# Strassen operand rings of their own, output weights loaded first, and attention's loads issued by POOL

## The chip, the cores and the metric

The kernel runs on one core of a Trainium2 chip. The metric is the device time of one execution in microseconds, as the median of several. One launch computes the whole block in float32. Engines are named as in the profile: PE (TensorE), DVE (VectorE), ACT (ScalarE), POOL (GpSimd), SP (SyncE, which here only issues DMAs).

## The reference

2048 rows of width 1024 pass through one block: normalization, one input projection to q, k, v (8 heads of 64) and u, vg, then stick-breaking attention beside a gated unit, normalization of each half, the output projection with a residual, and an MLP of width 4096 with squared relu.

```
h = rmsnorm(x, norm_mix_g);  q, k, v, u, vg = split(h @ w_in)
a_out = stick_breaking_attention(q, k, v)     # A[t,s] = sigmoid(z_ts) * prod_{s<j<t} (1 - sigmoid(z_tj))
b_out = spatial_gating(gelu(u), gelu(vg), sg_ln_g, sg_ln_b, sg_w, sg_b)
mix = concat(rmsnorm(a_out, g[:512]), rmsnorm(b_out, g[512:]))
x = x + mix @ w_out
x = x + square(relu(rmsnorm(x, norm_mlp_g) @ w_up)) @ w_down
return rmsnorm(x, norm_final_g)
```

## The kernel before

The rows are worked in four chunks of 512. Every float32 product is made of three passes: `split` (L78 to L85) turns an operand into a high part (ACT copies it, L81) and a low part (DVE subtracts, L82), and `mm3` (L87 to L91) issues high by high, high by low and low by high as 128 x 128 by 128 x 512 matmuls. These are called main matmuls below.

The stages follow each other: the projection of chunks 0 and 1 (to about 280 us), of chunks 2 and 3 (to 612), Out(0) and Out(1) (to 830), the up projection of chunks 0 and 1 by plain products (to 1340), Out(2) (to 1480), the plain down projection of chunks 0 and 1 with Out(3) beside its end (to 1930), and then chunks 2 and 3 by Strassen's seven products, up (to about 2262) and down (to the end).

Attention is a generator (`attention`, L316 to L411) that is dealt out beside the other stages by `together` at fixed rates, from 280 us on. It has 80 units (chunk, head, segment of keys) of four steps. Each step weighs one block (two score matmuls, L345 and L346, and on the diagonal a mask, L348; two sigmoids on ACT; a scan L359 and a product L360 on DVE), turns an earlier one (transposes L370 and a split) and gathers a still earlier one (value matmuls L388 and L389). At the first step of a unit it loads keys (two DMAs, L329), values (L331) and on the diagonal queries (L334), all issued by SP, into rings of 2, 3 and 2 buffers.

`Out` makes a chunk's output projection: `operands` (L465) loads attention's output a_d and the gated half b_d, takes both sums of squares, scales b's rows on ACT so that one factor serves both halves, and transposes b; `weights` (L506) loads a quarter of w_out, splits it and, for chunk 0, the product stores it split; `product` (L521) runs 8 x 3 main matmuls into each of 8 banks, which L543 adds to the residual; `turn` (L552) normalizes and transposes for the MLP.

In the Strassen part `Rights` and `Lefts` make the operands of the up products, and `down_seven` (L818 on) those of the down products: 4 groups of 7 products of 48 main matmuls; each product loads its left operand from s_d (L857), splits two left and two right operands and is added from four banks by L828, in the last group also by L831. All of these tiles, raw and split, share one ring `w8` of nine buffers; weights of odd groups take some of them too.

The scheduler fixes the order of each engine's and each queue's instructions when the kernel is built, from the order of the code, its own estimates and the buffers that are free. Each engine and each queue then runs in that order: what stands behind a waiting DMA on SP waits too.

Of the kernel before, what the change touches and what calls it, by code (L numbers as in the profile page):

```python
# [16 lines left out]
P = 128  # L17
# [17 lines left out]
def block_kernel(ctx: ExitStack, tc: tile.TileContext, x, x_t, gmix, w_in, ln_g, ln_b, sgw, sgb,  # L35
# [280 lines left out]
    def attention(cs):  # L316
# [4 lines left out]
        def weigh(u, tb):  # L321
# [4 lines left out]
            if tb == 0:  # L326
                kt = att.tile([P, 2, TC], F32R, name="kt", bufs=2)
                for j in range(2):
                    nc.sync.dma_start(kt[j * HD:(j + 1) * HD].bitcast(F32), k_d[h, :, :, ss].rearrange("x d t -> d x t"))  # L329
                vt = att.tile([P, NTB, 2 * HD], F32R, name="vt", bufs=3)  # L330
                nc.sync.dma_start(vt.bitcast(F32), v_d[seg, h].rearrange("p n x d -> p n (x d)"))  # L331
                if diag:
                    qt = att.tile([P, TC], F32R, name="qt", bufs=2)
                    nc.sync.dma_start(qt.bitcast(F32), q_d[h].rearrange("x d t -> (x d) t")[:, tcs])  # L334
                    carry = [None] * NTB
                else:
                    qt, carry = state[u - 1][2:4]
                state[u] = [kt, vt, qt, carry, []]
# [85 lines left out]
    class Room:  # L424
# [11 lines left out]

        def raw8(self, shape):
            return self.get("w8", shape)

# [19 lines left out]
    class Out:  # L459
# [5 lines left out]
        def operands(self):  # L465

            rm, c = self.rm, self.c
            at = rm.t8([4, TC])
            nc.sync.dma_start(at, a_d[:, c * TC:(c + 1) * TC].rearrange("(n p) t -> p n t", p=P))
            st = rm.t8([4, SBW])  # L470
            nc.sync.dma_start(st, b_d[c * TC:(c + 1) * TC, :].rearrange("(n p) d -> p n d", p=P))
            ssq = rm.small("rb_ssq", NTB)
            for tb in range(NTB):
                sq = rm.t4([SBW], BF16)
                nc.scalar.activation(sq, st[:, tb, :], AF.Square, accum_out=ssq[:, tb:tb + 1])
            am = self.am = rm.pair([4, TC])
            split4(am, at)
            yield
            nc.scalar.activation(at, at, AF.Square)
            total = rm.pool.tile([P, TC], F32, name="a_sq", bufs=1)  # L480
            nc.gpsimd.tensor_tensor(at[:, 0:2, :], at[:, 0:2, :], at[:, 2:4, :], ALU.add)
            nc.gpsimd.tensor_tensor(total, at[:, 0, :], at[:, 1, :], ALU.add)
            rb = rsqrt_mean(rm.pool, ssq, NTB, SBW, "rb")
            pssq = rm.ps()
            for tb in range(NTB):
                nc.tensor.matmul(pssq[:, tb:tb + 1], total[:, tb * P:(tb + 1) * P], ones, start=True, stop=True)
            m = rm.small("ra_m", NTB)
            nc.vector.tensor_scalar(m, pssq[:, :NTB], 1.0 / SBW, EPS, ALU.mult, ALU.add)
            ra = rm.small("ra", NTB)
            nc.gpsimd.tensor_tensor(ra, m, mhalf[:, :NTB], ALU.pow)  # L490
            root = rm.small("ra_root", NTB)
            nc.gpsimd.tensor_tensor(root, m, ra, ALU.mult)
            nc.gpsimd.tensor_tensor(rb, rb, root, ALU.mult)
            self.ras = [ra[:, tb:tb + 1] for tb in range(NTB)]
            yield
            bm = self.bm = rm.pair([4, TC])
            for tb in range(NTB):
# [6 lines left out]
                yield  # L504

        def weights(self, half, part):  # L506
# [14 lines left out]
        def product(self):  # L521
            rm, c = self.rm, self.c
            self.ys = []
            for t2 in range(2):
                y = rm.t8([2, D])
                r0 = c * TC + t2 * 2 * P
                nc.sync.dma_start(y, x[r0:r0 + 2 * P, :].rearrange("(n p) d -> p n d", p=P))
                self.ys += [y[:, 0, :], y[:, 1, :]]
            ys = self.ys

            for half in range(2):
                ws = [self.weights(half, part) for part in range(2)]
                hs = slice(half * 512, (half + 1) * 512)
                for tb in range(NTB):
                    ts_ = slice(tb * P, (tb + 1) * P)
                    ps = rm.ps()
                    for part, m in ((0, self.am), (1, self.bm)):
                        for e in range(4):
                            mm3(ps, m[0][:, e, ts_], m[1][:, e, ts_], ws[part][0][:, e, :], ws[part][1][:, e, :],
                                part == 0 and e == 0, part == 1 and e == 3)  # L540
                            if e == 1 or part == 0 and e == 3:
                                yield
                    nc.vector.scalar_tensor_tensor(ys[tb][:, hs], ps, self.ras[tb], ys[tb][:, hs], ALU.mult, ALU.add)  # L543
                    if half == 1:
                        nc.sync.dma_start(y_d[c][:, tb, :], ys[tb])
                    yield
                if c == 0:
                    for part in range(2):
                        for i in range(2):
                            nc.sync.dma_start(wo_d[half, part, i], ws[part][i].bitcast(F32))  # L550

# [124 lines left out]
    class Rights:  # L676


        def __init__(self, rm):

            self.rm, self.hc = rm, [None] * 7
            self.b11, self.t2, self.b12, self.b21, self.b22 = (rm.raw8([4, TC]) for _ in range(5))
# [28 lines left out]
    class Lefts:  # L711


        def __init__(self, rm, q):
            self.rm, self.pair, self.n = rm, None, 0
            st = rm.raw8([2, 2, 512])
# [77 lines left out]
    class Down:  # L794
# [260 lines left out]
```

## Time and profile before

| | us |
|---|---|
| median of 3 runs | 2624.02 |
| lowest and highest run | 2620.88, 2625.3 |
| the profiled execution | 2620.27 |
| its span | 2618.6 |
| busy: PE, DVE, ACT, POOL | 2454.1, 1684.6, 1158.5, 315.4 |

The span is the time from the first to the last instruction of the profiled execution; 1.7 us of its time lie around it. Busy time is what an engine's instructions cover. A matmul's record is longer than the distance to the next one, since they are pipelined.

### The profile page before, as it was taken

The page shows a single profiled execution, that of the slowest core. Times are in us where ns is not written, and L with a number is a line of the kernel's source. Part 1 is how long each engine was busy: PE and PEld are TensorE (multiplying, and loading weights), DVE is VectorE, ACT ScalarE, POOL GpSimd, SP SyncE. Part 2 cuts the span into 40 slices and gives each one's busy share as a digit, 9 for nine tenths or more (in the row PEclk, how much of TensorE's full clock was granted, in tenths as well). Part 3 has the DMA queues.
Part 4 walks back from the last instruction along what each step waited for, and adds up shares of the span by engine and source line. Part 5 has one row for each costly group of instructions (what it writes and reads, how often), then busy time and mean ns, then how long its engine had stood idle before and what let it go on. Part 6 is the DMA issues. An engine that isn't in the chain of part 4 may idle for free. (4 is left out here: it accounts for less than half of the span.)

```text
span 2618.6 us, 30138 instructions
## 1 busy us (share of the span) xinstructions
PE 2454.1 (94%) x11328; PEld 1985.7 (76%) x11328; DVE 1684.6 (64%) x2236; ACT 1158.5 (44%) x2020; POOL 315.4 (12%) x259
## 2 busy tenths in 40 slices
PE   8899898997979999999999899999989999799997
PEld 7787677775757888888877688788767888687875
DVE  3643557868675666666666688635566665468877
ACT  4422335536454555555564454313134544233333
POOL 1100000101010000000010000000023323213330
PEclk9999999998989999999999899999999999999998
DMA  9637788677654343333364633346223344753332
GB/s 374 244 125 219 215 255 261 205 221 224 244 190 157 121 121 121 121 124 122 121 236 162 197 121 113 122 156 241 96 81 142 140 161 149 261 206 116 113 113 113
DMA packets 158225, 446.58 MB, mean 171 GB/s; under 512 B 12544, under 2 KB 28928, under 8 KB 138624
## 3 DMA queue, kind: packets, MB, share of 16 engines
q1 hardware_dynamic: 149744, 417.39, 47.8%
q0 software_dynamic: 4032, 25.17, 2.4%
q10 hardware_dynamic: 4304, 2.10, 0.3%
q8 instruction: 90, 1.47, 0.2%
q14 instruction: 55, 0.45, 0.1%
HBM read 314.59 MB, written 130.02 MB: 170 GB/s over the span
## 5 line engine op out<-in xcount | busy, mean ns | idle before, releaser
L89 PE MATMUL mm<-t,t 128*128 128x512 f32 x1280 | 499.5, 394 | 4.5 <-DVE t L664 4.5
L91 PE MATMUL mm<-t,t 128*128 128x512 f32 x1280 | 502.3, 393 | 0.0
L90 PE MATMUL mm<-t,t 128*128 128x512 f32 x1280 | 501.9, 392 | 0.3 <-DVE t L82 0.3
L359 DVE TENSOR_TENSOR_SCAN pr<-kk,pr,zeros 128x513 f32<-128x513 f32 x192 | 248.3, 1293 | 117.3 <-ACT kk L351 116.9
L351 ACT ACTIVATE kk<-z 128x512 f32<-128x512 f32 (+2 forms) x320 | 171.5, 536 | 334.5 <-PE z L346 187.8
L89 PEld LDWEIGHTS mm<-t,t 128*128 128x128 f32 x1280 | 242.3, 190 | 55.6 <-DVE t L664 4.9
L90 PEld LDWEIGHTS mm<-t,t 128*128 128x128 f32 x1280 | 241.9, 189 | 51.4 <-DVE t L82 1.1
L91 PEld LDWEIGHTS mm<-t,t 128*128 128x128 f32 x1280 | 241.5, 189 | 51.6
L81 ACT ACTIVATE w<-w 128x512 fp32r<-128x512 f32 (+1 forms) x150 | 121.1, 825 | 299.6 <-DMA w<-s_d 172.3
L82 DVE TENSOR_TENSOR w<-w,w 128x512 fp32r<-128x512 f32 (+1 forms) x150 | 176.5, 1191 | 88.7 <-ACT w L81 86.8
L370 PE MATMUL tr<-ident,b 128*128 128x128 f32 x1088 | 186.3, 283 | 43.7 <-DVE aT L82 30.0
L90 PE MATMUL mm<-w,w 128*128 128x512 f32 x512 | 204.1, 399 | 17.3 <-DVE w L82 17.3
L82 DVE TENSOR_TENSOR aT<-tr,aT 128x512 fp32r<-128x512 f32 (+1 forms) x320 | 190.9, 599 | 35.7 <-ACT aT L81 35.6
L89 PE MATMUL mm<-w,w 128*128 128x512 f32 x512 | 201.4, 396 | 12.4 <-ACT w L81 11.5
L81 ACT ACTIVATE aT<-tr 128x512 fp32r<-128x512 f32 (+1 forms) x320 | 172.6, 541 | 90.2 <-PE tr L370 89.7
L91 PE MATMUL mm<-w,w 128*128 128x512 f32 x512 | 202.8, 396 | 0.0
L370 PEld LDWEIGHTS tr<-ident,b 128*128 128x128 f32 x1088 | 133.6, 144 | 90.7 <-DVE aT L82 38.8
L81 ACT ACTIVATE t<-t 128x1024 fp32r<-128x1024 f32 x104 | 105.7, 1060 | 179.1 <-DMA t<-in_w_down 112.8
L353 ACT ACTIVATE b<-z 128x512 f32<-128x512 f32 (+2 forms) x320 | 171.3, 535 | 0.5 <-PE tr L370 0.5
L356 DVE TENSOR_TENSOR_SCAN pr<-kk,zeros 128x128 f32<-128x128 f32 (+3 forms) x128 | 105.5, 826 | 90.8 <-ACT kk L351 90.3
L89 PE MATMUL mm<-t,w 128*128 128x512 f32 x384 | 154.0, 401 | 8.9 <-DVE acts L775 4.7
L388 PE MATMUL av<-aT,vt 128*128 128x512 f32 (+1 forms) x320 | 144.5, 452 | 13.7 <-DMA vt<-v_d 3.5
(192 smaller groups left out, 4629.3 us busy)
## 6 DMA issues: line engine op xcount, KB each, us to landing
w_in<-wi_d SPq DMA_DIRECT2D x40, 1024.0 KB, 8.0
kt<-k_d SPq DMA_DIRECT2D x160, 256.0 KB, 4.9
t<-in_w_down SPq DMA_DIRECT2D x28, 1024.0 KB, 6.6
s_d<-acts SPq DMA_DIRECT2D x16, 1792.0 KB, 6.2
w<-s_d SPq DMA_DIRECT2D x28, 1024.0 KB, 4.8
t<-wo_d SPq DMA_DIRECT2D x24, 1024.0 KB, 8.7
wi_d<-w_in POOLq DMA_DIRECT2D x20, 1024.0 KB, 8.0
vt<-v_d SPq DMA_DIRECT2D x80, 256.0 KB, 2.9
```

What stands on the lines that cost most here:

```text
L81: nc.scalar.activation(hi, src, AF.Copy)
L82: nc.vector.tensor_tensor(lo, src, hi.bitcast(F32), ALU.subtract)
L89: nc.tensor.matmul(ps, lh, rh, start=first, stop=False, skip_group_check=more)
L90: nc.tensor.matmul(ps, lh, rl, start=False, stop=False, skip_group_check=more)
L91: nc.tensor.matmul(ps, ll, rh, start=False, stop=last, skip_group_check=more)
L351: nc.scalar.activation(kk[:, :L], z[:, :L], AF.Sigmoid, scale=-QK_SCALE)
L353: nc.scalar.activation(b[:, :L], z[:, :L], AF.Sigmoid, scale=QK_SCALE)
L356: nc.vector.tensor_tensor_scan(pr[:, L - 1::-1], kk[:, L - 1::-1], zeros[:, :L], 1.0, ALU.mult, ALU.add)
L359: nc.vector.tensor_tensor_scan(pr[:, ::-1], kk[:, ::-1], zeros, carry[tb], ALU.mult, ALU.add)
L370: nc.tensor.transpose(tr[:, tb * P:(tb + 1) * P], bs[tb][:, j * P:(j + 1) * P], ident)
L388: nc.tensor.matmul(av[:, t0:], vt[:, j, :], aT[:, 0, t0:], start=first, stop=False)
```

## The change

Three edits, and all that the scheduler makes of them.

Attention's loads go from `nc.sync` to `nc.gpsimd`. In `Out`, the first quarter of the weights is loaded before the operands, b is transposed as it is and its row factors are applied at the eviction, so that the product has four groups of four banks (half 0 of b, half 0 of a, half 1 of b, half 1 of a); a's sum of squares is taken by 16 small matmuls instead of additions on POOL and 4 of them. In the Strassen part the ring of nine becomes three: `w8` of 5, `raw8` of 2 for loads that are still to be split, and `x8` of 2.

```diff
@@ attention, weigh
-                    nc.sync.dma_start(kt[j * HD:(j + 1) * HD].bitcast(F32), k_d[h, :, :, ss].rearrange("x d t -> d x t"))
+                    nc.gpsimd.dma_start(kt[j * HD:(j + 1) * HD].bitcast(F32), k_d[h, :, :, ss].rearrange("x d t -> d x t"))
...
-                nc.sync.dma_start(vt.bitcast(F32), v_d[seg, h].rearrange("p n x d -> p n (x d)"))
+                nc.gpsimd.dma_start(vt.bitcast(F32), v_d[seg, h].rearrange("p n x d -> p n (x d)"))
...
-                    nc.sync.dma_start(qt.bitcast(F32), q_d[h].rearrange("x d t -> (x d) t")[:, tcs])
+                    nc.gpsimd.dma_start(qt.bitcast(F32), q_d[h].rearrange("x d t -> (x d) t")[:, tcs])
@@ Room
-        def raw8(self, shape):
-            return self.get("w8", shape)
+        def raw8(self, shape, dtype=F32):
+            return self.get("raw8", shape, dtype)
+
+        def x8(self, shape, dtype=F32R):
+            return self.get("x8", shape, dtype)
@@ Out.operands
+            self.rbs = []
+            self.ready = [self.weights(0, 1)]
+            st = rm.t8([4, SBW])
+            nc.sync.dma_start(st, b_d[c * TC:(c + 1) * TC, :].rearrange("(n p) d -> p n d", p=P))
...
+                m = rm.small("rb_m", NTB)
+                nc.vector.tensor_scalar(m, ssq, 1.0 / SBW, EPS, ALU.mult, ALU.add)
+                rb = rm.small("rb", bufs=2 * NTB)
+                nc.gpsimd.tensor_tensor(rb, m, mhalf[:, 0:1], ALU.pow)
+                self.rbs.append(rb)
...
-            nc.gpsimd.tensor_tensor(at[:, 0:2, :], at[:, 0:2, :], at[:, 2:4, :], ALU.add)
-            nc.gpsimd.tensor_tensor(total, at[:, 0, :], at[:, 1, :], ALU.add)
...
-                nc.scalar.activation(st[:, tb, :], st[:, tb, :], AF.Copy, scale=rb[:, tb:tb + 1])
...
+            for tb in range(NTB):
+                for e in range(4):
+                    nc.tensor.matmul(pssq[:, tb:tb + 1], at[:, e, tb * P:(tb + 1) * P], ones, start=e == 0, stop=e == 3)
+            ra = rsqrt_mean(rm.pool, pssq[:, :NTB], NTB, SBW, "ra")
@@ Out.product
+            def group(half, part, m, rr):
+                ws = self.ready.pop() if self.ready else self.weights(half, part)
...
+                    for e in range(4):
+                        mm3(ps, m[0][:, e, ts_], m[1][:, e, ts_], ws[0][:, e, :], ws[1][:, e, :], e == 0, e == 3)
...
+                    nc.vector.scalar_tensor_tensor(ys[tb][:, hs], ps, rr[tb], ys[tb][:, hs], ALU.mult, ALU.add)
...
+            yield from group(0, 1, self.bm, self.rbs)
+            yield from group(0, 0, self.am, self.ras)
+            yield from group(1, 1, self.bm, self.rbs)
+            yield from group(1, 0, self.am, self.ras)
@@ Rights
-            self.keep(0, b11, rm.w8)
+            self.keep(0, b11, rm.x8)
@@ Lefts.operand
-                self.pair = self.rm.w8([2, 2, 512])
+                self.pair = self.rm.raw8([2, 2, 512], F32R) if self.first and self.n == 0 else self.rm.w8([2, 2, 512])
@@ Down.load
-                    st = self.rm.raw8([4, 512]) if g % 2 and h else self.rm.t8([4, 512])
+                    st = self.rm.x8([4, 512], F32) if g % 2 and h else self.rm.t8([4, 512])
@@ block_kernel
-    rm = Room(None, None, dict(w8=9, s12=1, t8=12, acts=2, t2=2), dict(w8=hx, s12=hx))
+    rm = Room(None, None, dict(w8=5, raw8=2, x8=2, s12=1, t8=12, acts=2, t2=2),
+              dict(w8=hx, raw8=hx, x8=hx, s12=hx))
```

PE, in the projection of chunk 2, at attention's fourth to sixth step (a name is the tile written, then the tiles read; z are scores, tr the transposes, av the values, mm a main bank). Before:

```order
L388 MATMUL av<-aT,vt 128x256
L389 MATMUL av<-aT,vt 128x256
L345 MATMUL z<-kt,qt 128x256
L346 MATMUL z<-kt,qt 128x256
L348 LDWEIGHTS ident_b
L348 MATMUL z<-neg_b,ident_b 128x128
L345 MATMUL z<-kt,qt 128x256
L346 MATMUL z<-kt,qt 128x256
```

With the change, two steps on:

```order
L348 LDWEIGHTS ident_b
L348 MATMUL z<-neg_b,ident_b 128x128
L370 MATMUL tr<-ident,b 128x128 x4
L388 MATMUL av<-aT,vt 128x256
L389 MATMUL av<-aT,vt 128x256
L89 MATMUL mm<-hT,w_in 128x512
L90 MATMUL mm<-hT,w_in 128x512
L91 MATMUL mm<-hT,w_in 128x512
```

Before, the score matmuls of one step follow those of the last with no main matmul between, and 64 of them come in one block after the eighth step; now 12 stand in most steps (here the first three of six, the other six behind the next step's scores). Counted over the whole order: of the 80 steps that lie beside the projection, 35 had none or almost none and 8 have none now; of the 49 up to the end of Out(1) it is 43 and 33; of those about Out(2) it is 17 and 23.

SP, at the seam between the Strassen stages (s_d are the left operands of the down products, stored by L587 or L586; in_w_down its weights; y_d the residual). Before, buffer numbers kept:

```order
L857 DMA w_18012<-s_d_97 128x2048
L808 DMA t_17985<-in_w_down 128x4x512
L587 DMA s_d_100<-acts 128x7x512
L808 DMA t_17987<-in_w_down 128x4x512
L808 DMA t_17989<-in_w_down 128x4x512
L808 DMA t_17991<-in_w_down 128x4x512
L819 DMA t_18001<-y_d_89 128x2048
L587 DMA s_d_100<-acts 128x7x512
L819 DMA t_18002<-y_d_89 128x2048
L819 DMA t_18005<-y_d_90 128x2048
L819 DMA t_18006<-y_d_90 128x2048
L857 DMA w_18088<-s_d_97 128x2048
```

With the change:

```order
L856 DMA raw_18144<-s_d_97 128x2048
L586 DMA s_d_100<-acts 128x7x512
L856 DMA raw_18220<-s_d_97 128x2048
L807 DMA x_18634<-in_w_down 128x4x512
L586 DMA s_d_100<-acts 128x7x512
L807 DMA t_18117<-in_w_down 128x4x512
L807 DMA t_18119<-in_w_down 128x4x512
L807 DMA t_18121<-in_w_down 128x4x512
L807 DMA t_18123<-in_w_down 128x4x512
L818 DMA t_18133<-y_d_89 128x2048
L586 DMA s_d_100<-acts 128x7x512
L818 DMA t_18134<-y_d_89 128x2048
```

Before, one load of a down product's operand (from s_d_97) stands ahead of the weights and y, now two, with one load of group 1's weights (x_18634) behind them.

DVE, in the first half of the Strassen down stage (w are split operands, raw the loaded ones; L828 or L827 adds a finished product's four banks). Before, buffer numbers kept:

```order
L82 TENSOR_TENSOR w_18598<-acts,w_18598 128x1024
L82 TENSOR_TENSOR w_18655<-w_18653,w_18655 128x1024
L82 TENSOR_TENSOR w_18658<-t_18498,w_18658 128x1024
L82 TENSOR_TENSOR w_18662<-w_18653,w_18662 128x1024
L82 TENSOR_TENSOR w_18665<-w_18502,w_18665 128x1024
L828 TENSOR_TENSOR t_18009<-mm,t_18009 128x512 x4
L82 TENSOR_TENSOR w_18727<-w_18721,w_18727 128x1024
```

With the change:

```order
L82 TENSOR_TENSOR w_18657<-x_18634,w_18657 128x1024
L82 TENSOR_TENSOR w_18721<-raw_18715,w_18721 128x1024
L82 TENSOR_TENSOR w_18724<-acts,w_18724 128x1024
L82 TENSOR_TENSOR w_18727<-raw_18715,w_18727 128x1024
L827 TENSOR_TENSOR t_18141<-mm,t_18141 128x512 x4
L82 TENSOR_TENSOR w_18730<-acts,w_18730 128x1024
L82 TENSOR_TENSOR w_18787<-raw_18785,w_18787 128x1024
L82 TENSOR_TENSOR w_18790<-t_18630,w_18790 128x1024
```

Before, the number of splits between one product's additions and the next's varies, and often all four of the next product stand ahead of the additions; now the additions of a product always stand ahead of the fourth split of the next.

## Rows read from the trace of the kernel before

**Rows 1.** The page, part 1: engine, busy us, share of the span, instructions.
```profile
PE 2454.1 (94%) x11328; PEld 1985.7 (76%) x11328; DVE 1684.6 (64%) x2236; ACT 1158.5 (44%) x2020; POOL 315.4 (12%) x259
```

**Rows 2.** Six stretches: ends and length, busy us of PE, PEld, DVE, ACT, POOL, clock, DMA share, GB/s.
```profile
280.00:480.00 200.00, 178.12 (x853) 138.10 (x852) 129.96 (x233) 92.38 (x201) 15.97 (x20) 0.97 0.79 244
480.00:612.00 132.00, 128.92 (x661) 105.88 (x661) 95.92 (x148) 59.45 (x123) 5.59 (x5) 1.00 0.70 204
612.00:830.00 218.00, 181.43 (x847) 140.05 (x846) 148.36 (x216) 110.84 (x224) 21.14 (x23) 0.89 0.65 217
830.00:1340.00 510.00, 507.37 (x2496) 417.40 (x2495) 334.94 (x425) 293.14 (x555) 12.79 (x13) 1.00 0.40 123
1340.00:1480.00 140.00, 119.64 (x575) 92.87 (x574) 98.83 (x128) 68.42 (x130) 9.36 (x11) 0.94 0.67 229
2262.00:2300.00 38.00, 22.09 (x73) 16.72 (x72) 20.07 (x18) 10.32 (x12) 16.47 (x7) 0.73 0.69 267
```

**Rows 3.** PE timeline at 662 us: start, duration, instruction.
```profile
661.97 0.39 PE L89 MATMUL mm<-t,t 128*128 128x512 f32 x1
662.20 0.39 PE L90 MATMUL mm<-t,t 128*128 128x512 f32 x1
```

**Rows 4.** Groups by line and shape, DVE: busy us, mean ns, idle before.
```profile
L359 DVE TENSOR_TENSOR_SCAN pr<-kk,pr,zeros 128x513 f32<-128x513 f32 x192 | 248.3, 1293 | 117.3 <-ACT kk L351 116.9
L82 DVE TENSOR_TENSOR aT<-tr,aT 128x512 fp32r<-128x512 f32 x224 | 152.4, 681 | 25.5 <-ACT aT L81 25.4
L360 DVE TENSOR_TENSOR b<-b,pr 128x512 f32<-128x512 f32 x192 | 132.9, 692 | 10.7
```

**Rows 5.** PE waits of 612 to 830 us: total us, times, longest.
```profile
PE mm L501 <- ACT t L498: 4.1, 4, 1.5
...
PE mm L486 <- POOL a_sq L482: 2.0, 1, 2.0
```

**Rows 6.** PE timeline at 637 us; below it the DVE group of the product's eviction.
```profile
637.30 0.95 PE L486 MATMUL mm<-ones,a_sq 128*128 128x1 f32 x8
L543 DVE SCALAR_TENSOR_TENSOR t<-mm,ra,t 128x512 f32<-128x512 f32 x32 | 24.0, 749 | 67.8 <-PE mm L91 60.2 <-issue 7.7
```

**Rows 7.** PE waits of 1340 to 1480 us.
```profile
PE av L388 <- DMA vt<-v_d: 3.5, 1, 3.5
```

**Rows 8.** PE waits of 2262 to 2300 us, and of 2300 to 2618 us.
```profile
PE mm L89 <- ACT w L81: 11.5, 1, 11.5
PE mm L90 <- DVE w L82: 12.9, 6, 7.3
```

**Rows 9.** SP timeline at the seam: start, duration, DMAs issued.
```profile
2236.96 0.34 SPq L857 DMA_DIRECT2D w<-s_d  x1
...
2250.15 6.90 SPq L808 DMA_DIRECT2D t<-in_w_down  x3
...
2272.64 2.99 SPq L819 DMA_DIRECT2D t<-y_d  x3
2275.68 25.96 SPq L857 DMA_DIRECT2D w<-s_d  x3
```

**Rows 10.** Groups by line and shape, DVE in the Strassen stages.
```profile
L82 DVE TENSOR_TENSOR w<-w,w 128x1024 fp32r<-128x1024 f32 x70 | 103.6, 1493 | 61.0 <-ACT w L81 61.0
...
L828 DVE TENSOR_TENSOR t<-mm,t 128x512 f32<-128x512 f32 x104 | 67.5, 684 | 16.5 <-PE mm L91 16.5
```

**Rows 11.** Queue waits of SP, whole span: total us, times, longest.
```profile
SPq L331 <- PE av L389: 330.2, 52, 12.6
```

**Rows 12.** POOL groups by line, and page part 6: KB each, us to landing.
```profile
L126 POOL DMA_DIRECT2D wi_d<-w_in x20 | 11.0, 551 | 133.0 <-DVE w_in L82 133.0
w_in<-wi_d SPq DMA_DIRECT2D x40, 1024.0 KB, 8.0
...
wi_d<-w_in POOLq DMA_DIRECT2D x20, 1024.0 KB, 8.0
```

More of the change, by code (lines that the diff above doesn't have):

```diff
@@ L467, in operands @@
             rm, c = self.rm, self.c
+            self.rbs = []
+            self.ready = [self.weights(0, 1)]
+            st = rm.t8([4, SBW])
+            nc.sync.dma_start(st, b_d[c * TC:(c + 1) * TC, :].rearrange("(n p) d -> p n d", p=P))
             at = rm.t8([4, TC])
             nc.sync.dma_start(at, a_d[:, c * TC:(c + 1) * TC].rearrange("(n p) t -> p n t", p=P))
-            st = rm.t8([4, SBW])
-            nc.sync.dma_start(st, b_d[c * TC:(c + 1) * TC, :].rearrange("(n p) d -> p n d", p=P))
@@ L472, in operands @@
-            ssq = rm.small("rb_ssq", NTB)
+            bm = self.bm = rm.pair([4, TC])
             for tb in range(NTB):
                 sq = rm.t4([SBW], BF16)
[L475 to L480, printed above, removed]
-            nc.gpsimd.tensor_tensor(at[:, 0:2, :], at[:, 0:2, :], at[:, 2:4, :], ALU.add)
@@ L482, in operands @@
-            nc.gpsimd.tensor_tensor(total, at[:, 0, :], at[:, 1, :], ALU.add)
[L483 to L497, printed above, removed]
-                nc.scalar.activation(st[:, tb, :], st[:, tb, :], AF.Copy, scale=rb[:, tb:tb + 1])
+                ssq = rm.small("rb_ssq")
+                nc.scalar.activation(sq, st[:, tb, :], AF.Square, accum_out=ssq)
@@ L499, in operands @@
+                m = rm.small("rb_m")
+                nc.vector.tensor_scalar(m, ssq, 1.0 / SBW, EPS, ALU.mult, ALU.add)
+                rb = rm.small("rb", bufs=2 * NTB)
+                nc.gpsimd.tensor_tensor(rb, m, mhalf[:, 0:1], ALU.pow)
+                self.rbs.append(rb)
                 ps = rm.ps((P, 4, P))
@@ L504, in operands @@
                 yield
+            am = self.am = rm.pair([4, TC])
+            split4(am, at)
+            nc.scalar.activation(at, at, AF.Square)
+            pssq = rm.ps()
+            for tb in range(NTB):
+                for e in range(4):
+                    nc.tensor.matmul(pssq[:, tb:tb + 1], at[:, e, tb * P:(tb + 1) * P], ones, start=e == 0, stop=e == 3)
+            ra = rsqrt_mean(rm.pool, pssq[:, :NTB], NTB, SBW, "ra")
+            self.ras = [ra[:, tb:tb + 1] for tb in range(NTB)]
+            yield
         def weights(self, half, part):
@@ L529, in product @@
             ys = self.ys
-            for half in range(2):
-                ws = [self.weights(half, part) for part in range(2)]
+            def group(half, part, m, rr):
+                ws = self.ready.pop() if self.ready else self.weights(half, part)
                 hs = slice(half * 512, (half + 1) * 512)
@@ L536, in product @@
                     ps = rm.ps()
[L537 to L544, printed above, removed]
+                    for e in range(4):
+                        mm3(ps, m[0][:, e, ts_], m[1][:, e, ts_], ws[0][:, e, :], ws[1][:, e, :], e == 0, e == 3)
+                        if e == 1:
+                            yield
+                    nc.vector.scalar_tensor_tensor(ys[tb][:, hs], ps, rr[tb], ys[tb][:, hs], ALU.mult, ALU.add)
+                    if half == 1 and part == 0:
                         nc.sync.dma_start(y_d[c][:, tb, :], ys[tb])
@@ L547, in product @@
                 if c == 0:
-                    for part in range(2):
-                        for i in range(2):
-                            nc.sync.dma_start(wo_d[half, part, i], ws[part][i].bitcast(F32))
+                    for i in range(2):
+                        nc.sync.dma_start(wo_d[half, part, i], ws[i].bitcast(F32))
+            yield from group(0, 1, self.bm, self.rbs)
+            yield from group(0, 0, self.am, self.ras)
+            yield from group(1, 1, self.bm, self.rbs)
+            yield from group(1, 0, self.am, self.ras)
         def turn(self):
@@ L681, in __init__ @@
             self.rm, self.hc = rm, [None] * 7
-            self.b11, self.t2, self.b12, self.b21, self.b22 = (rm.raw8([4, TC]) for _ in range(5))
+            self.b11, self.t2, self.b12, self.b21, self.b22 = (rm.get("w8", [4, TC]) for _ in range(5))
             b11 = self.b11
@@ L714, in __init__ @@
         def __init__(self, rm, q):
-            self.rm, self.pair, self.n = rm, None, 0
+            self.rm, self.pair, self.n, self.first = rm, None, 0, q == 0
             st = rm.raw8([2, 2, 512])
```

## The prediction

> **What bounds the kernel now.** I read the page's busy shares first, then the stretches, then PE's waits in the stretches that fall short. PE is busy for 94% of the span and the next engine, DVE, for 64% [rows 1], so only what PE still loses can be won. The stretches show where that is: in the plain up projection (830 to 1340 us) PE is idle for 2.6 of 510 us at a clock of 1.00, while 280 to 480 loses 21.9, 612 to 830 loses 36.6, 1340 to 1480 loses 20.4 and the seam at 2262 loses 15.9, the last three at a clock of 0.94 and less [rows 2].
>
> The good stretch explains the bad ones. The main matmuls follow each other by 0.23 us [rows 3]. In the good stretch each step of attention has 12 of them beside it, 12 x 0.227 = 2.7 us of work. A step's own chain on DVE is 1.29 + 0.69 + 0.68 = 2.67 us [rows 4]; a step's matmuls fill about 1.2 us of PE (its two score matmuls, four transposes and two value matmuls, at the same spacing by columns). With 12 main matmuls beside it a step is hidden. Without any ("alone") PE waits for up to 2.67 - 1.2 = 1.45 us. What matters is thus how evenly the built order deals main matmuls to the steps, and the order of before and of the change can be counted.
>
> **The change part by part.** The sum is against the profiled execution, 2620.3 us; the median of the runs shown, 2624.0, stands 3.7 above it, and I add that at the end.
>
> *Loads of keys, values and queries on POOL, projection of chunks 2 and 3 (280 to 612 us).* 272 issues leave SP. On SP a load of values waits at the head of the queue until PE has released a buffer: 52 waits, 330 us in all, 6.3 each [rows 11], and the projection's weights stand behind it. In the order of before, 35 of these 80 steps are alone, with blocks of 22 to 64 main matmuls between; in the changed order 8 are, and nearly all the others have 6, 12 or 18. By step count 27 x 1.45 = 39 us; by what the stretch loses, 21.9 idle plus 200 x (1 - 0.97) = 6 of clock, of which 27 in 35 go, 22. The second is a cap as far as busy time is PE at its peak, which in interrupted stretches it is not. I take **-24** (ends -39 and -12, the latter if half of the lost time has other causes).
>
> *Out(0) and Out(1) (612 to 830).* Before has 43 alone steps there, the change 33. The stretch loses 36.6 idle and 218 x 0.11 = 24 of clock [rows 2], 1.4 for an alone step, so 10 fewer are worth -14. The raw transposes of b no longer wait for ACT's scaled copy, nor the sum of squares for POOL's additions: 4.1 + 2.0 us [rows 5], -6. Added: the sum of squares takes 16 matmuls instead of 4; four took 0.95 us [rows 6], so +2.85 for each Out, +5.7 for two. Each Out has 16 evictions instead of 8, 0.75 us each [rows 6], hidden under the 12 matmuls (2.7 us) of each bank; uncovered, the sixteen more in two Outs would cost 12, and I charge 3. Weights come first and on a free queue, which is in the step count already. Sum **-11** (ends -20 and +6).
>
> *Out(2) (1340 to 1480).* Here the changed order is worse: 23 alone steps against 17. The stretch loses 20.4 + 140 x 0.06 = 28.8 us over 17, 1.7 each: +10. Added matmuls +2.85, the wait for values on a late load goes, -3.5 [rows 7], and some of the scaling wait, -2. Sum **+7** (0 to +15). *Out(3)*, beside the plain down projection, keeps its cover: **+3** (0 to +6), the added matmuls.
>
> *The seam (2262 to 2300).* PE stands still for 11.5 us [rows 8]. SP tells why: it issues one load of the first down products at 2236.96, then the weights and y, and only from 2275.7 the next, the last at the end of a run of three that takes 26 us [rows 9]. With a ring of two for raw loads, two stand ahead of weights and y in the changed order. The 11.5 go; the third load still stands behind the same list, now longer by one weight load, and I charge 2.5 for it. **-9** (ends -14 and -3).
>
> *Strassen down with a ring of five (2300 to the end).* Each product splits four operands into the ring. With five buffers the fourth can be written only after the product before has ended, and DVE first adds that one's four banks: 4 x 0.68 + 1.49 = 4.2 us [rows 10]. The fourth operand is wanted after half of a product's 48 matmuls, 24 x 0.227 = 5.5 us in. So it fits by 1.3 us in the regular products. It does not in the last group, where 8 to 12 further additions of 0.7 stand between (about 5 us each for three products, +15), and the 12.9 us which PE waits there now [rows 8] are about half of the same kind, -7. **+8** (ends -4 and +25).
>
> Sum: -24 - 11 + 7 + 3 - 9 + 8 = -26, so 2594.3 profiled and **2598** as a median.
>
> *A rule against the change.* POOL's issue took 0.55 us, and 1 MB moved by its queue landed in 8.0 us, as long as one of SP's [rows 12]. The Trainium skill (DMA: Bandwidth & Descriptors, section Issuing engine by pattern) says that the sync and scalar path "is generally faster", and its section SWDGE vs HWDGE vs iDMA that GpSimd's descriptors go to rings in SBUF that VectorE can lock it out of. Those two rows show no such delay, though they were taken with little of DVE's work beside them. By the row a moved load costs nothing; by the rule it comes later, which is the third rival's matter.
>
> **The rivals.**
> *The ring of five stalls every product: slower.* Beside POOL's own additions a split takes longer than its mean, and if the fourth operand were wanted at the 12th matmul (2.7 us), all 27 seams between products would lose 4.2 - 2.7 = 1.5 us: +40 instead of +8, **2630**. It decides from the point at which adds and split pass 5.5 us. For it: the place where the split stands in the order. Against it: 1.3 us of slack by the means.
> *Even order gains nothing: no change.* If attention's chain on DVE rather than the dealing set the time, -24 would be 0: **2622**. For it: DVE's 2.67 us a step almost equals 12 matmuls. Against it: the plain up projection runs the same chain with PE at 507 of 510 us.
> *POOL's queue becomes the wait.* Between the loads on POOL stand the norms' small powers. A load of values that waits 6.3 us [rows 11] now holds those up instead of SP's loads. About 40 powers stand in the stretches of Out(0) to Out(2); if the path meets 4 of them whole, +25: **2623**; if 6, slower. For it: POOL's order has them in turns. Against it: the values each load waits for are read on PE two steps or more ahead of the power's use. By the two sections of the Trainium skill's DMA: Bandwidth & Descriptors named above the loads themselves would come late as well; the time is this rival's.
>
> **How the numbers follow.** Two runs of this kernel differ by some 0.2%, 5.2 us, so "the same" is 2618.8 to 2629.3. The forecast has a chance of 0.82, the ring 0.07, even order 0.06, POOL's queue 0.05. The forecast's ends, taken together as independent, reach about 23 below and 29 above, 2575 to 2627; little more than 1 in 10 on each side may be left out, so the range is **2573 to 2624**, which takes in the second and third rivals. Faster 0.78 (the forecast but for 0.04 above 2618.8), the same 0.12 (that 0.04, even order, 0.02 of POOL's queue), slower 0.10 (the ring and the rest of POOL's queue).
>
> **What would show it.** Right: in 280 to 480 us (now earlier at its end) PE idles for under 8 us and its clock is 1.00; a plain run of 12 main matmuls per step; SP's queue no longer waits for PE's value matmuls and POOL's does; the 11.5 us at the seam gone; Out(2) idle by more than 20 us; waits of PE for a DVE split of 4 to 6 us in the last group alone. Wrong: a PE wait for DVE in each of the down products; VectorE waits for POOL's powers; loads of keys that PE's score matmuls wait for.

## The result and the profile after

The change takes 2597.04 us in the median (2596.54 to 2598.17, 4 runs) against 2623.05 (2620.88 to 2625.3, 4 runs), a ratio of 0.9901 (95% interval 0.9884 to 0.9919). 2598 was forecast. The sum was right; the largest term and two others were not, and they cancelled.

The page of the kernel after, part 1, in the columns of [rows 1]:

```profile
PE 2465.3 (95%) x11424; PEld 2009.5 (77%) x11424; DVE 1709.3 (66%) x2280; ACT 1150.7 (44%) x2004; POOL 473.4 (18%) x527
```

The two profiled executions stand 2.8 us below and 1.1 above their medians, so of the 26.0 us between the medians they show 22.1. Milestones say where these (by the spans, 2618.6 and 2596.5) lie. PE's timeline of the kernel before (start, duration, instruction), at the last matmul of the projection, the last of the plain up projection, the first of Strassen up, the first and the last of Strassen down:

```profile
609.58 0.40 PE L91 MATMUL mm<-w_in,hT 128*128 128x512 f32 x1
...
1342.97 0.40 PE L91 MATMUL mm<-t,t 128*128 128x512 f32 x1
...
1936.15 0.50 PE L89 MATMUL mm<-w,w 128*128 128x512 f32 x1 [0.82 <-DVE t L664]
...
2262.83 0.40 PE L89 MATMUL mm<-w,w 128*128 128x512 f32 x1
...
2607.05 0.39 PE L91 MATMUL mm<-w,w 128*128 128x512 f32 x1
```

The same five places in the kernel after:

```profile
612.00 0.40 PE L91 MATMUL mm<-w_in,hT 128*128 128x512 f32 x1
...
1337.86 0.40 PE L91 MATMUL mm<-t,t 128*128 128x512 f32 x1
...
1931.28 0.39 PE L89 MATMUL mm<-x,raw 128*128 128x512 f32 x1
...
2256.13 0.40 PE L89 MATMUL mm<-w,w 128*128 128x512 f32 x1
...
2583.49 0.39 PE L91 MATMUL mm<-w,w 128*128 128x512 f32 x1
```

| part | forecast | measured, by the differences of these rows |
|---|---|---|
| to the end of the projection | -24 | 612.0 - 609.6 = +2.4 |
| Out(0), Out(1), up projection | -11 | -5.1 - 2.4 = -7.5 |
| Out(2), plain down projection, Out(3) | +10 | -4.9 + 5.1 = +0.2 |
| Strassen up | 0 | -6.7 + 4.9 = -1.8 |
| seam, Strassen down, what follows it | -1 | -22.1 + 6.7 = -15.4 |

Why did the projection gain nothing? PE's waits from 254 to 612 us of the kernel before (total us, times, longest):

```profile
PE tr L370 <- DVE b L357: 9.5, 15, 1.5
PE mm L89 <- DMA w_in<-wi_d: 6.0, 4, 2.4
PE tr L370 <- DVE aT L82: 4.4, 4, 1.6
...
PE av L388 <- DVE ao L398: 1.1, 1, 1.1
...
PE z L345 <- DMA qt<-q_d: 0.6, 2, 0.4
```

And of the kernel after:

```profile
PE mm L89 <- DMA w_in<-wi_d: 18.2, 10, 4.5
PE z L345 <- DMA qt<-q_d: 5.9, 1, 5.9
PE av L388 <- DVE ao L398: 4.5, 4, 2.0
...
PE tr L370 <- DVE aT L82: 1.0, 2, 0.5
```

The waits for attention's chain on DVE went as forecast, from 9.5 + 4.4 to 1.0. In their place PE waits for the projection's weights, for the first queries and for the gathered heads: 28.6 us in all, where these three had 7.7.

SP's own waits from 280 to 612 us show why the weights did not come earlier with these loads off the queue. Before, of the 330 us that loads of values wait in the whole span [rows 11], only 25.4 lie here; the loads of weights (L121) wait as long until PE has left a tile of their ring:

```profile
SPq L121 <- PE mm L91: 27.3, 8, 7.1
SPq L331 <- PE av L389: 25.4, 5, 12.0
```

After, with the loads of values gone, they wait longer for their tiles, and land 9.8 us after their issue in the median, where it was 8.0 [rows 12]:

```profile
SPq L121 <- PE mm L91: 65.0, 12, 23.2
```

At the seam SP's timeline of the kernel after (beside [rows 9]) has two loads of the down operands and one of group 1's weights (x) ahead of the four weights, and the next two operands behind y:

```profile
2216.50 0.34 SPq L856 DMA_DIRECT2D raw<-s_d  x1
...
2235.76 0.33 SPq L856 DMA_DIRECT2D raw<-s_d  x1
2239.60 0.37 SPq L807 DMA_DIRECT2D x<-in_w_down  x1
...
2242.56 8.39 SPq L807 DMA_DIRECT2D t<-in_w_down  x4
...
2270.72 5.71 SPq L856 DMA_DIRECT2D raw<-s_d  x2
```

PE's waits from 2240 to the end, before:

```profile
PE mm L90 <- DVE w L82: 17.3, 7, 7.3
PE mm L89 <- ACT w L81: 11.5, 1, 11.5
```

and after:

```profile
PE mm L90 <- DVE w L82: 9.0, 8, 3.5
PE mm L89 <- ACT w L81: 3.1, 3, 1.7
```

The 11.5 of [rows 8] is gone, and the waits for DVE's splits have halved where the forecast had them grow. Counted in PE's order by products of 48 matmuls, the first three products of the stage take 9.8 us less than before, the other 25 take 7.1 less, and what follows the last matmul takes 1.5 more.

### The profile page after: what moved, and what is told of

Same layout as the page of the kernel before. It is cut to its first block, busy times and chain, and to the rows that moved or that the text cites. A ratio compares the mean times of both kernels' runs of the same rounds, so it can differ in the third digit from the quotient of the medians.

```text
span 2596.5 us, 30413 instructions
## 1 busy us (share of the span) xinstructions
PE 2465.3 (95%) x11424; PEld 2009.5 (77%) x11424; DVE 1709.3 (66%) x2280; ACT 1150.7 (44%) x2004; POOL 473.4 (18%) x527
## 4 chain that ended last, share of the span: by engine, by line
PE 76%; DVE 9%; DMA 9%; issue 3%; ACT 2%; POOL 1%; SPq 0%; POOLq 0%; ACTq 0%; DVEq 0%
PE mm L91 21%; PE mm L90 21%; PE mm L89 21%; PE tr L370 4%; DMA w_in<-wi_d 3%; PE av L388 2%; PE av L389 2%; PE z L346 2%; PE z L345 2%; DVE w L82 2%; DMA t<-in_w_down 1%; DVE pr L359 1%; DMA v_d<-qkv_st 1%; PE mm L498 1%; DMA stx<-in_x_t 1%
## 5 line engine op out<-in xcount | busy, mean ns | idle before, releaser
L359 DVE TENSOR_TENSOR_SCAN pr<-kk,pr,zeros 128x513 f32<-128x513 f32 x192 | 246.8, 1285 | 124.1 <-ACT kk L351 123.8
L82 DVE TENSOR_TENSOR aT<-tr,aT 128x512 fp32r<-128x512 f32 (+1 forms) x320 | 191.4, 598 | 15.6 <-ACT aT L81 15.4
L370 PE MATMUL tr<-ident,b 128*128 128x128 f32 x1088 | 179.2, 279 | 16.5 <-DVE aT L82 16.4
L331 POOL DMA_DIRECT2D vt<-v_d x80 | 46.4, 580 | 805.0 <-PE av L389 800.7
L90 PE MATMUL mm<-w,w 128*128 128x512 f32 x448 | 178.2, 398 | 10.6 <-DVE w L82 9.0
L91 PE MATMUL mm<-w,w 128*128 128x512 f32 x448 | 176.9, 395 | 0.0
L89 PE MATMUL mm<-w,w 128*128 128x512 f32 x448 | 173.0, 392 | 3.1 <-ACT w L81 3.1
L82 DVE TENSOR_TENSOR w<-raw,w 128x512 fp32r<-128x512 f32 (+1 forms) x135 | 152.7, 1132 | 3.4 <-ACT w L81 3.0
L89 PE MATMUL mm<-t,w 128*128 128x512 f32 x380 | 151.5, 399 | 2.7 <-ACT w L81 2.3
L91 PE MATMUL mm<-t,w 128*128 128x512 f32 x380 | 150.3, 396 | 1.9 <-DVE w L82 1.9
```

The lines of the kernel that those rows point to most:

```text
L82: nc.vector.tensor_tensor(lo, src, hi.bitcast(F32), ALU.subtract)
L89: nc.tensor.matmul(ps, lh, rh, start=first, stop=False, skip_group_check=more)
L90: nc.tensor.matmul(ps, lh, rl, start=False, stop=False, skip_group_check=more)
L91: nc.tensor.matmul(ps, ll, rh, start=False, stop=last, skip_group_check=more)
L359: nc.vector.tensor_tensor_scan(pr[:, ::-1], kk[:, ::-1], zeros, carry[tb], ALU.mult, ALU.add)
L370: nc.tensor.transpose(tr[:, tb * P:(tb + 1) * P], bs[tb][:, j * P:(j + 1) * P], ident)
```

## The experiments

**The three parts alone, and the change without the first.** Each run is compared with the kernel before, timed on the same chip.

```diff
# run e1: the kernel before, with
-                    nc.sync.dma_start(kt[...
+                    nc.gpsimd.dma_start(kt[...
# and the same for vt and qt
```

> Edit: before, with attention's loads of keys, values and queries issued by POOL and nothing else. The order deals the projection's matmuls evenly (7 alone steps of the 79 beside it, as in the change, against 32), but has 46 and 29 alone steps about Out(0), Out(1) and Out(2) (before 44 and 16). Theory A (the even order exchanges waits for DVE for waits for the projection's weights, so it gains nothing): the projection of chunks 2 and 3 ends within 4 us of before's 610, PE waits there for w_in grow from 6 to 15 us or more, and 13 more alone steps about Out(2) cost some 15: 2625 to 2640. Theory B (the even order is worth the forecast's 24 us): the projection ends at about 586, and the time is 2600 to 2615.

Measured: 2623.96 against 2622.12, ratio 1.0009 (1.0000 to 1.0019). The projection's last matmul starts at 619.1, 9.5 us later than before and so later than theory A allowed, and PE waits 23.8 us for w_in there, as theory A said. Theory B is out. The time still came out under theory A's range: from the end of the plain up projection to Strassen up, where the 13 alone steps more about Out(2) stand, only 2.2 us are lost and not 15, and Out(0) and Out(1) take 7.6 us less than before. Alone, this part gains nothing.

```diff
# run e2: the kernel before, with the change's Out.operands and Out.product
```

> Edit: before, with the new Out (weights first, b transposed unscaled, four groups) and nothing else. The order has 35 and 13 alone steps about Out(0), Out(1) and Out(2), against 44 and 16 before. Theory A (an alone step costs about 1.4 us and the 48 small matmuls more in four Outs 11): -17 + 11 = -6, 2617. Theory B (the additional evictions and matmuls are paid in full and the alone steps cost nothing): 2632 or more.

Measured: 2611.16, ratio 0.9964 (0.9951 to 0.9977): -11.0 us, more than the -6 of theory A, and theory B is out.

```diff
# run e3: the kernel before, with
-    rm = Room(None, None, dict(w8=9, s12=1, t8=12, acts=2, t2=2), dict(w8=hx, s12=hx))
+    rm = Room(None, None, dict(w8=5, raw8=2, x8=2, s12=1, t8=12, acts=2, t2=2),
+              dict(w8=hx, raw8=hx, x8=hx, s12=hx))
# and the tiles that go to raw8 and x8 in the change
```

> Edit: before, with the three rings in the Strassen part and nothing else. Theory A (read from the two traces: the Strassen stages end 17 us earlier after their own start, 6 to 9 at the seam, the rest in the down stage's last group): 2606, with a PE wait at the seam of under 5 us and no PE wait over 4 us behind it. Theory B (the forecast: seam -9, ring of five +8): 2622.

Measured: 2593.45, ratio 0.9897 (0.9883 to 0.9912): -28.7 us. The rings alone are worth as much as the whole change (0.9897 and 0.9901, with intervals that overlap). Theory B, the forecast, is out by 29 us; theory A was still 13 short.

```diff
# run e4: the change, with
-                    nc.gpsimd.dma_start(kt[...
+                    nc.sync.dma_start(kt[...
# and the same for vt and qt
```

> Edit: the change, with attention's loads issued by SP again (new Out and the three rings stay). The order has 32, 35 and 13 alone steps in the three places, against 7, 34 and 22 with POOL. Theory A (POOL's loads gain nothing in the projection and cost by the alone steps about Out(2)): 2585 to 2597, as fast as the change or faster by up to 12. Theory B (POOL's loads are worth the forecast's 24): 2615 to 2622.

Measured: 2586.90, ratio 0.9869 (0.9854 to 0.9885), -35.2 us where the change has -26.0. Without its first part the change is some 10 us faster, so theory A holds. The projection's last matmul starts at 611.8, as in the change (612.0): beside the projection POOL's loads neither gain nor cost. The trace puts the gap (11.0 us by the spans, 2585.5 and 2596.5) in two places.

Strassen up starts at 1924.5 instead of 1931.3. These 6.8 us open between 1421 and 1517 us of the kernel after, behind Out(2)'s product, where it has 9 alone steps more: PE waits there 7.2 us for keys and 3.7 in e4, and its granted clock is 0.91 and 0.94.

Strassen down, from its first matmul to the end of the span, takes 335.0 instead of 340.4. Attention is long over there, but 2.9 of the 5.4 us still come from its loads: the span goes on for 4.1 us behind the last landing of the output, in e4 for 1.2. The end waits for a drain of POOL's queue. The instructions of the kernel's last line (count, then shortest, median and longest in ns), in the kernel after:

```profile
L1051 POOLq DRAIN  x3: 45/93/7852, 2587.8 to 2596.2; - x3
```

In e4 and in the kernel before the longest takes 2.9 us; in e1, e5 and e11, where POOL issues attention's loads too, 7.9. The other 2.5 us lie between the first and the last matmul, where PE is busy for 2.4 us longer over the same matmuls, at a granted clock of 0.98 against 0.99; why it falls further was not tried.

**Is it the weights that end the projection?** Two runs leave out half of the weights' traffic.

```diff
# run e5: the change; run e6: the kernel before; in weights(col)
+            if cs[0] > 0:
+                two = [weight(col, k2) for k2 in range(2)]
+                return two + two
             return [weight(col, k2) for k2 in range(KD // 2)]
```

> Edit: the change, with two instead of four tiles of weights loaded for each column of chunks 2 and 3; the matmuls read these two twice, so half of the projection's weights for these chunks is left out and half of that traffic goes; PE's work is the same. The order has no alone step beside the projection (the change 7). Theory A (in the change PE waits there for weights, 18 us, and those waits took the place of the ones for DVE): the waits for w_in fall below 5 us, the projection ends at 585 to 597 instead of 612, and the time is 2575 to 2585. Theory B (DVE's chain of attention sets the pace of these stretches, the weights only look late): it ends at 608 or later, 2592 to 2597.

> Edit: the same half of the weights left out in the kernel before. The order has 12 alone steps beside the projection (before 32), since the freed buffers let the scheduler deal more evenly, with SP's loads. Theory A (weights set the pace): ends at 590 to 600, 2605 to 2612, and by the 12 alone steps up to 17 us later than the other kernel with half the weights. Theory B (DVE's chain sets it): 605 or later, 2615 to 2623.

Measured: 2568.28 (ratio 0.9798, 0.9781 to 0.9816) and 2601.70 (0.9924, 0.9907 to 0.9940). The last matmuls of the projection, of e5 and then of e6, by PE's timeline:

```profile
589.20 0.40 PE L91 MATMUL mm<-w_in,hT 128*128 128x512 f32 x1
```

```profile
588.09 0.40 PE L91 MATMUL mm<-w_in,hT 128*128 128x512 f32 x1
```

Both end 21 to 23 us sooner, and in neither is a wait of PE for w_in left in the list. Both times came out below theory A's ranges: with the weights early the forecast's 24 us are there to be had. e5 shows that in the change the weights set the end, for the change's order was nearly even already (7 alone steps, e5 none). e6 does not part the two causes, since its order has 12 alone steps where before has 32, and part of its 21 us may be the dealing. What it shows beside e5 is that, with the weights early, 12 alone steps cost nothing there; I had allowed 17 us.

**Bytes or buffers, and POOL or SP.** To part the transfer from the ring of five tiles, the bytes were halved with the number of tiles kept.

```diff
# run e11: the change, for chunks 2 and 3 (lo is 0 there)
-                nc.sync.dma_start(w.bitcast(F32), wi_d[col, k2])
+                nc.sync.dma_start(w[:, 0].bitcast(F32), wi_d[col, k2, :, 0])
...
-                        mm3(ps, w[:, 0, k % 2, es], w[:, 1, k % 2, es], h[:, 0, k % 2, :], h[:, 1, k % 2, :],
+                        mm3(ps, w[:, 0, k % 2, es], w[:, lo, k % 2, es], h[:, 0, k % 2, :], h[:, 1, k % 2, :],
# run e12: the same, with attention's loads on nc.sync
```

> Edit: the change, with only the high half of each reloaded tile of weights brought in for chunks 2 and 3 (512 KB instead of 1 MB, the same number of tiles in the same ring of five), and the matmul with the low half reading the high half again; the low part of these weights is left out, PE's work is the same. The order has 1 alone step beside the projection. Theory A1 (the bytes set the projection's end: PE waits for transfers): w_in waits fall from 18 us to under 6, the projection ends at 588 to 596, 2570 to 2580. Theory A2 (the ring's release sets it: a tile can only be asked for when PE has left the last one): waits of 12 us or more stay, it ends at 606 or later, 2590 to 2597.

> Edit: as the run before, with attention's loads on SP. The order has 16, 35 and 13 alone steps, against 1, 34 and 22 with POOL. Theory A (once the weights are early, the dealing beside the projection still gains nothing): the projection ends within 4 us of the run before, and by the 9 alone steps fewer about Out(2) the time is 5 to 10 us less. Theory B (with the weights early an alone step costs its 1.4 us): it ends 15 to 22 us later than there, and the time is 5 to 17 us more.

Measured: 2586.02 (ratio 0.9861, 0.9844 to 0.9878) and 2569.09 (0.9801, 0.9785 to 0.9817). The projection's last matmul starts at 603.5 in e11, between the two theories' times: half the bytes in as many tiles bring 8.6 us, half the bytes in half the tiles (e5) 22.8. PE's waits in e11, from 254 to 612 us:

```profile
PE mm L89 <- DMA w_in<-wi_d: 7.2, 5, 3.3
PE av L388 <- DVE ao L398: 5.4, 3, 3.8
PE z L345 <- DMA qt<-q_d: 5.3, 1, 5.3
```

and in e12:

```profile
PE av L388 <- DVE ao L398: 4.4, 3, 3.5
PE mm L89 <- DMA w_in<-wi_d: 4.3, 3, 2.2
...
PE z L345 <- DMA qt<-q_d: 1.4, 1, 1.4
```

With SP's loads and 16 alone steps the projection ends at 593.1, 10.3 us before POOL's loads with one alone step. That rules out theory B of e12, and goes further than its theory A: here POOL's loads, or the order that comes with them, cost. Of the 10.3, 3.9 are the wait for queries, 2.9 that for weights, 1.0 that for the heads; the clock of 280 to 480 us is 0.97 in e11 and 0.99 in e12, some 4 us; waits for attention's splits take 1.5 back.

The ring's own share is not shown. With e11's bytes in e11's five tiles e12 ends within 4 us of e5, so most of what parts e11 from e5 goes with the loads' queue and the order.

**Is it the queue that the weights stand in?**

```diff
# run e10: the change with attention's loads on nc.sync, and in weight(col, k2)
-                nc.sync.dma_start(w.bitcast(F32), wi_d[col, k2])
+                nc.gpsimd.dma_start(w.bitcast(F32), wi_d[col, k2])
```

> Edit: the change with attention's loads on SP, and in their place the projection's reloaded weights (w_in, 20 loads of 1 MB for chunks 2 and 3, and as many before) issued by POOL. The order has 2, 35 and 13 alone steps in the three places, so even dealing beside the projection without the loss about Out(2). Theory A (the weights' buffers and transfers set the projection's end, not the queue that issues them, nor the dealing): the projection ends at 608 or later, PE waits there for w_in 15 us or more, 2583 to 2590. Theory B (weights were late because they stood in SP's queue behind stores and attention's loads): waits for w_in under 6 us, the projection ends at 590, 2563 to 2570.

(These are 40 loads, 20 for each chunk.) Measured: 2592.87, ratio 0.9890 (0.9873 to 0.9907), 6 us over e4, a little above theory A's range. The last matmul starts at 615.2. PE waits 12.1 us for w_in, fewer than the 15 of theory A, and besides 8.6 us for a split of the normalized rows and 5.3 ahead of a score matmul, which theory A did not have. In a queue of their own the loads of weights still wait for their tiles, by POOL's waits from 254 to 612 us:

```profile
POOL w_in L121 <- PE mm L91: 159.2, 28, 30.6
```

Theory B is out: with two alone steps and a queue of their own the weights end the projection no earlier.

**Which ring?**

```diff
# run e7: the kernel before, with raw loads alone in a ring of their own
+    rm = Room(None, None, dict(w8=7, raw8=2, s12=1, t8=12, acts=2, t2=2),
# run e8: the kernel before, with only the tiles of x8 in a ring of their own
+    rm = Room(None, None, dict(w8=7, x8=2, s12=1, t8=12, acts=2, t2=2),
```

> Edit: before, with only the raw loads of the Strassen part in a ring of their own (raw8 of 2, w8 of 7 for everything else, the tiles of x8 among it). Theory A (the gain of 29 comes from loads that no longer wait in one ring with the split operands): 2591 to 2600, the seam's wait under 5 us. Theory B (it comes from the odd groups' weights leaving the ring): the seam's gain alone, 2610 to 2616.

> Edit: before, with only the odd groups' weights (and the first right operand) in a ring of their own (x8 of 2), raw loads and split operands sharing w8 of 7. Theory A (the raw loads' own ring is the gain): 2616 to 2630, the wait of 11.5 us at the seam stays. Theory B (the weights' own ring is the gain): 2600 to 2608.

Measured: 2597.23 (ratio 0.9905, 0.9879 to 0.9932) and 2614.08 (0.9974, 0.9964 to 0.9983), -24 and -7 us. From the first to the last matmul of Strassen down e7 takes 323.6 us, e8 339.2 and e3 324.3, before 344.2: the raw loads' ring alone has all that the rings gain there, and the two parts do not add. PE's waits from 2240 us on, e7:

```profile
PE mm L90 <- DVE w L82: 9.9, 6, 4.3
PE mm L89 <- ACT w L81: 1.3, 2, 1.1
```

and e8:

```profile
PE mm L89 <- ACT w L81: 13.0, 2, 12.9
PE mm L90 <- DVE w L82: 11.9, 3, 7.8
```

The long wait at the seam and the one of over 7 us in the last group both go with the raw loads' own ring, and stay without it. Theory A holds, except that the other ring gives some 7 us too, which it did not allow.

**The 12 small matmuls more.**

```diff
# run e9: the change with attention's loads on nc.sync, and in Out.operands
+            nc.gpsimd.tensor_tensor(at[:, 0:2, :], at[:, 0:2, :], at[:, 2:4, :], ALU.add)
+            nc.gpsimd.tensor_tensor(total, at[:, 0, :], at[:, 1, :], ALU.add)
...
-                for e in range(4):
-                    nc.tensor.matmul(pssq[:, tb:tb + 1], at[:, e, tb * P:(tb + 1) * P], ones, start=e == 0, stop=e == 3)
+                nc.tensor.matmul(pssq[:, tb:tb + 1], total[:, tb * P:(tb + 1) * P], ones, start=True, stop=True)
```

> Edit: the change with attention's loads on SP (2586.9 measured), and a's sum of squares taken as before by two additions on POOL and 4 matmuls instead of 16. The order has 32, 35 and 14 alone steps, as without this edit. Theory A (the forecast's term: 12 more matmuls cost 2.85 us in each Out, and nothing hides them): 2576 to 2579. Theory B (they stand in stretches where PE waits for DVE anyway, and POOL's two additions of 2.4 and 1.6 us come back as a wait): 2585 to 2590.

Measured: 2575.63, ratio 0.9828 (0.9813 to 0.9842), 11.3 us under e4. That is theory A's size, 4 x 2.85 = 11.4, but the trace does not bear out its reason. The 2.85 was read where the granted clock was 1.00 [rows 6]; the runs of 16 stand mostly at 0.50, the lower of the clock's two levels (1.2 GHz). PE's timeline of the kernel after at Out(0) and Out(3) (the profile has two records for each of these matmuls):

```profile
646.15 6.83 PE L498 MATMUL mm<-ones,t 128*128 128x1 f32 x32
...
1710.23 4.33 PE L498 MATMUL mm<-ones,t 128*128 128x1 f32 x32
```

The four runs take 25.2 us in e4 and 5.8 in e9. Against these 19.4, POOL's additions come back as waits, 4.7 us from 612 to 860 us of e9 and 2.6 at Out(3):

```profile
PE mm L500 <- POOL a_sq L497: 4.7, 2, 2.7
```

From the end of the projection to Strassen up, which holds all four sums, PE idles for 56.1 us in e9 and 43.5 in e4, and the stretch is only 3.7 us shorter. The profiled executions lie 7.4 us apart, the medians 11.3; where the rest comes from is open, so the agreement with 11.4 is in part luck.

Of the versions that leave no work out this is the fastest: the rings and the new Out, with the sum on POOL and attention's loads on SP.

## Why the forecast held, and where it did not

*The projection, -24.* The failed step is the cap: "by what the stretch loses, 21.9 idle plus ... 6 of clock, of which 27 in 35 go". I counted that all lost time was the alone steps' and that nothing stood behind it. The waits for DVE did go, but the weights were nearly as late as the steps: their 6.0 us of waits were in the list of before, and the stretch's DMA share of 0.79 is the highest of the six [rows 2]. The waits that the weights were to be freed from I read over the whole span [rows 11]; 25.4 of those 330 us lie here. The reading that fits: before, steps that ran alone filled PE's time until weights came; dealt evenly they no longer do, and PE waits for the weights instead. e5 shows that the weights then set the end; how much of that is their bytes and how much the ring is open. The second rival, even order gains nothing, named this outcome, but with another cause: DVE's chain, which e5 rules out, for the chain is the same there and the projection ends at 589.

*Out(0) and Out(1), -11.* -7.5 measured, with the up projection; inside its ends. The scaling wait is gone. The term for the small matmuls was too small: their two runs take 6.83 and 6.82 us, where before they took 0.95 [rows 6] and 1.87, so +10.8 and not +5.7. The price came from one run at a clock of 1.00, and these runs stand at 0.50.

*Out(2) and Out(3), +10.* +0.2, inside the ends of the two terms, at the low one. The 1.7 for an alone step was too high, and no one price fits: 9 of them go with 6.8 us between e4 and the change, 13 with 2.2 in e1. The small matmuls of these two Outs cost +8.8 instead of 5.7. A wait that I had only as a sign of being wrong is in the 6.8: PE waits 6.1 us for keys at Out(2); its timeline, and POOL's:

```profile
1455.87 0.77 PE L345 MATMUL z<-kt,qt 128*128 128x512 f32 x1 [6.13 <-DMA kt<-k_d]
```

```profile
1450.04 0.59 POOL L329 DMA_DIRECT2D kt<-k_d  x1 [4.51 <-PE z L346]
```

The load is issued when a score matmul has released its buffer and lands 5.8 us later, and the next score matmul waits for it. In a run of 18 alone steps no main matmul covers that.

*The seam, -9.* PE was idle for 15.9 us of 2262 to 2300 before [rows 2] and is for 6.8 after (38 less 31.16 busy). The mechanism and the size were right (-9.8 by the first three products), and e7 and e8 pin it to the raw loads' ring.

*The ring of five, +8.* This has the wrong sign: the other 25 products take 7.1 us less, and PE's waits for splits behind 2300 us fell from 12.9 [rows 8] to 4.8. The failed step is "The fourth operand is wanted after half of a product's 48 matmuls, 24 x 0.227 = 5.5 us in". In the last group the change has the very row of additions that I feared. DVE's timeline:

```profile
2520.37 1.37 DVE L827 TENSOR_TENSOR t<-mm,t 128x512 f32<-128x512 f32 x2 [0.16 <-PE mm L91]
2521.66 4.38 DVE L830 TENSOR_TENSOR t<-t,t 128x512 f32<-128x512 f32 x6
...
2527.16 3.69 DVE L830 TENSOR_TENSOR t<-t,t 128x512 f32<-128x512 f32 x6
2530.77 1.22 DVE L82 TENSOR_TENSOR w<-x,w 128x1024 fp32r<-128x1024 f32 x1
```

PE's timeline beside it:

```profile
2527.65 1.07 PE L89 MATMUL mm<-w,w 128*128 128x512 f32 x4
2528.97 1.21 PE L89 MATMUL mm<-w,w 128*128 128x512 f32 x4 [0.24 <-ACT w L81]
2532.04 0.72 PE L90 MATMUL mm<-w,w 128*128 128x512 f32 x1 [1.86 <-DVE w L82]
```

The split ends 11.6 us after the additions began, as reckoned. But they began 1.8 us before this product did (2522.2), and PE's order takes eight matmuls that need only high parts first, so that it asks for the low part 8.0 us into the product and waits for 1.9, the longest wait for a split behind the seam; 15 were charged for three such products. I took the place of the demand from the code instead of from PE's order.

*The rivals.* The ring's +40 did not come: no wait for a split over 3.5 us is left. POOL's queue as the wait came in part, some 10 us by e4: as waits for keys about Out(2) and as POOL's drain at the end, not for the norms' powers. The rule of the Trainium skill (DMA: Bandwidth & Descriptors, section Issuing engine by pattern) can be weighed now. The kernel after, part 6 of its page:

```profile
kt<-k_d POOLq DMA_DIRECT2D x160, 256.0 KB, 5.0
...
vt<-v_d POOLq DMA_DIRECT2D x80, 256.0 KB, 3.1
```

Keys landed 4.9 and values 2.9 us after their issue by SP's queue. Over all runs values take 3.0 to 3.2 us by POOL and 2.7 to 3.0 by SP, keys 4.7 to 5.0 and 4.8 to 5.0. So the traces agree as to the sign for values alone, by some 0.2 us, which is too little to be the 10 us.

Of the signs named beforehand, the queues and the seam came as said. PE still idles for 17.6 us of 280 to 480, at a clock of 0.97, where under 8 at 1.00 would have shown the projection's term right; and one sign of being wrong came, loads of keys that score matmuls wait for.

So the forecast's time was right by 1 us while its account was not: the projection fell 26 us short of its term, and the Strassen down stage (14 better) and Out(2) (10 better) made it good. A right sum of wrong terms is luck; the milestones show it at once.

## What to carry to other kernels

A stretch's lost time belongs to the wait that ends last in it, and taking that away gives only what lies above the next one: read the second line of the waits, here weights at 6.0 us, before crediting the first. A queue's waits, too, are read in the stretch itself and not over the whole span. Loads that wait to be worked on did better here in a ring of their own than in one with the results (e7, 24 us with as many buffers in all); the likely reason, not shown apart, is that in a shared ring a load's place comes up only when the results before it are done with. A small instruction is priced at the clock of the place where it will stand. And when an operand is wanted is read from the consumer's order, not from the loop that writes it.

## What the runs showed of the hardware that was not expected

The queue from which the loads were issued made little difference to one load: values took 3.1 us by POOL's queue and 2.9 by SP's. It made one to the end of the kernel: with 272 loads more by POOL its last drain takes 7.9 us and not 2.9, in all four kernels that have them, and the span ends 4.1 us behind the last landing and not 1.1 to 1.4 (e10, with 40 loads of weights by POOL: 6.2 and 2.5). A POOL issue of such a load takes 0.58 us. DVE's scan was no slower beside 272 issues of POOL: 1285 ns against the 1293 of [rows 4].

A run of one-column matmuls did not hold TensorE's clock. At Out(3) of the kernel after, main matmuls follow each other right up to the 32 records of the sum at a granted clock of 1.00; within the 4.33 us of these the clock falls to 0.50, though PE is never idle, and the main matmuls behind them take 0.63 us a record and not 0.39.
